# Opening an attention layer by scale alone: the norm's root and the shift moved behind the first six products

## The chip, the core and the metric

The kernel runs on one core of a Trainium2 chip. Its engines work side by side, each through its own list of instructions in order: TensorE (PE, matrix products into PSUM), VectorE (DVE), ScalarE (ACT), GpSimd (POOL), and SyncE (SP), which issues the DMAs of this kernel. The metric is the device time of one execution in microseconds (us); lower is better. The profile of one execution names every instruction by engine, line of the kernel, operation and tile.

## The reference

The model has two layers over 512 latent tokens and 256 context tokens of width 1024: grouped-query attention (16 query heads, 4 key heads, head dimension 64), then a gated feed-forward with a convolution, then a Mamba-2 style mixer, then another feed-forward. The change lies in the first few per cent of the time, at the start of the attention layer, where this is computed (cut to what matters):

```python
def rms_norm(x, g):                       # root over the 1024 features of a token
    return x * lax.rsqrt(jnp.mean(x * x, axis=-1, keepdims=True) + EPS) * g
def modulate(x, shift, scale):
    return x * (1 + scale) + shift
# shift, scale, gate: SiLU(cond) through a linear map of the layer (adaLN);
# latents use c, context tokens use c_ctx
h_lat = modulate(rms_norm(x,   g), shift_c,    scale_c)
h_ctx = modulate(rms_norm(ctx, g), shift_cctx, scale_cctx)
q_l, k_l, v_l = split(h_lat @ w_qkv)      # queries and keys are then normed per head (q_norm, k_norm)
q_c, k_c, v_c = split(h_ctx @ w_qkv)      # and the latents' rotated by position
```

All of it is in float32. For one token, with root r, gain a = g (1 + scale) and shift b, both vectors over the features: h = r (a x) + b, and so h W = r ((a x) W) + b W. The first form is what the kernel before computes; the second is what the changed kernel computes for the first six tiles of keys and queries.

## The kernel before

**Layout.** Features lie on the 128 partitions, tokens along the free axis. X holds the stream as eight feature tiles of 128 x 768 (512 latents, then 256 context tokens). A float32 product is made as three fp32r products (`mm3`, lines 104, 105 and 107): high part of the weight by high part of the activation, high weight by low activation, low weight by high activation. So every operand is first split: the high part is a copy rounded to fp32r, the low part is the difference. For weights `split` does it (L85 on ACT, L87 on DVE or POOL), for activations `modulated` does (L321 on DVE: x times gain times root into `ht`; L330 on ACT: plus shift, rounded, the high part; L331 on DVE: the low part). With `pool=True` it is L326 and L327 on ACT and L328 on POOL instead of the last two.

**The opening** is in `attention()`. There a block under `manual_schedule` (L523 to L639) keeps PE, ACT and DVE in the order in which the code is written. First X is loaded (L1570), the squares are summed (L574 on ACT, L576 on DVE), and `rstd_rows` makes the root of each token and spreads it over the partitions (from L274 on). Only then come eight steps, one per feature tile m. Step m needs

- the shift and the gain of tile m: `ada` multiplies 1 MB of adaLN weights (DMA `wada`, products `ps_ada` L128), copies them (`ada_sb`, L130), turns them (`ps_adt`, L134), and `modulation` makes `mod` (L145, shift and scale) and `moda` (L148, gain times one plus scale);
- a slab of weights, 128 x 768 (DMA into `wst`, then `wsh` on ACT L85 and `wsl` on POOL L87, the last on DVE);
- the two halves `hha`, `hla` of the modulated latents of tile m.

Then 18 products of 512 columns add tile m to six PSUM tiles `ps_l`: two tiles of keys and the first four of queries. From m = 4 on, two tiles of the context are modulated behind each step's latents (`pool=True`), with a root made at m = 3 and 4 from `sqc`.

**Behind the opening** the order is set by the priorities of the program rather than by hand. The six `ps_l` are copied to `raw` (L646, ACT). Six context products `ps_c` of 24 instructions each follow with the same slabs, each copied behind the latents' columns of `raw` (L863). A finished `raw` tile goes through the head norm and the rotation: squares `qsq` (L671, ACT), norm weight (L672, ACT), four small DMAs `qsw` that swap pairs (L675), sums `ssq` (L680, PE), cosine and sine (L682 to L684, DVE), root (L689 to L691, ACT), L693 to L695 (DVE). Then keys and queries are split, the values `ps_v` (L660) and the first score maxima `ps_m` (L764) are computed, and the heads follow one after the other for the rest of the layer. The values and the later queries read the same modulated latents `hha`, `hla`.

Of the kernel before, what the change touches and what calls it, by code (L numbers as in the profile page):

```python
# [7 lines left out]
P = 128  # L8
# [7 lines left out]
D = 1024  # L16
# [36 lines left out]
_col("cc", 2 * KT)  # L53
_col("qn", 1)
_col("kn", 1)
# [240 lines left out]

def parts(x, a=0, b=1 << 30):
# [217 lines left out]
def attention(g, adas, project, X):  # L515
# [6 lines left out]
    g.h = [[htiles(g, n, f"a{i}_{m}") for m in range(KT)] for i, n in enumerate((L, C))]  # L522
    hl, hc = g.h  # L523
# [32 lines left out]
    nc.sync.dma_start(g.cst, I["cst"][:, :CST_COS])  # L556
    for m in range(1, 5):
        next(mods[m])
        next(loads[m])
        if m == 2:  # L560
            for a in range(0, KT, 4):
                nc.sync.dma_start(X[:, a : a + 4, L:], I["ctxT"][a * P : (a + 4) * P].rearrange("(k p) t -> p k t", p=P))
# [7 lines left out]
    busy(38)  # L570
    acc = t3(g, "acc", n=L)
    for m in range(KT):
        sq = t2("sql") if m else acc
        nc.scalar.activation(sq, xs[0][m], AF.Square)  # L574
# [14 lines left out]
    next(norm)  # L589
    next(mods[0])  # L590
    busy(8)
    rsl, _, _ = next(norm)
    next(mods[0])
    next(loads[0], None)
    busy(3)
    modulated(g, hl[0], xs[0], rsl, 0, L, 0, 1, 0, 0, 0)
    rs_ps, rsl = rsl, t3(g, "rsl", n=L)
    nc.scalar.copy(rsl, rs_ps)
# [7 lines left out]
    for m in range(KT):  # L606
# [3 lines left out]
        if m == 1:  # L610
            sqc = t3(g, "sqc", n=C)
# [1121 lines left out]
```

## Time and profile before

| what | us |
|---|---|
| median of 3 runs | 1885.04 |
| lowest and highest of them | 1882.46, 1888.78 |
| the profiled execution's own time | 1889.8 |
| its span from first to last instruction | 1888.0 |
| PE busy in the span | 1862.3 |

The granted clock of TensorE is 0.995 of full speed over that execution. The profiled execution lies 4.8 us above the median of the runs, so a length read in the trace is compared with the profiled execution's own time, and differences are carried over to the median. In the rows of a timeline the first number is the start in us from the start of the span, the second the length; then come engine, line, operation, output and inputs with their shapes and the count. In square brackets stands the time the engine idled just before, and what ended it.

The opening runs until about 65 us, the context products until about 89 us, and the first score maxima start at 96.31 us. All that follows, 95% of the time, is the same code in both kernels, but for two details: the context's tiles now hold both halves in one tile, and the second mixer loads its input into tiles of that size.

### The profile page before, as it was taken

Reading aid. Unit: us, or ns where it says so; the run is one execution under the profiler, and the core shown is the slowest. Engines: PE = TensorE matmul, PEld = TensorE weight load, DVE = VectorE, ACT = ScalarE, POOL = GpSimd, SP = SyncE. Lnnn points to the kernel's source line nnn. Section 1 sums busy time; section 2 is a strip of 40 time slices with the busy share of each in tenths; the row PEclk is TensorE's granted clock in tenths of the full one; section 3 lists DMA queues with packets and bytes.
Section 4 is the critical chain, followed back from the end, with each engine's and each line's share of the span. In section 5 each row is a group of like instructions: output and inputs, shape, how many; then the busy total and the mean of one; then the engine's idle time right before and its main releaser. Section 6 shows DMA issues by size and latency. Waiting matters only on the chain.

```text
span 1888.0 us, 27471 instructions
## 1 busy us (share of the span) xinstructions
PE 1862.3 (99%) x10794; PEld 1535.3 (81%) x10794; DVE 1346.3 (71%) x2013; ACT 832.8 (44%) x1422; POOL 251.8 (13%) x220
## 2 busy tenths in 40 slices
PE   9999999999999999999999999999999999999999
PEld 7865555689888888888898888888887888888887
DVE  5688899678777777444478977777888576565655
ACT  3655544354122222222256677766667352323331
POOL 2100000030000000000030435454434200000000
PEclk9999999989999999999999999999999999999999
DMA  9223241024443555222223344343344323323232
GB/s 342 68 83 114 89 145 62 2 78 145 156 124 121 171 188 167 68 68 67 80 77 106 91 123 133 104 133 123 108 129 136 97 74 105 101 83 107 90 101 90
DMA packets 73489, 210.02 MB, mean 111 GB/s; under 512 B 8976, under 2 KB 14480, under 8 KB 73232
## 3 DMA queue, kind: packets, MB, share of 16 engines
q1 hardware_dynamic: 73360, 208.26, 34.8%
q8 instruction: 85, 1.39, 0.3%
q14 instruction: 44, 0.36, 0.1%
HBM read 198.79 MB, written 6.82 MB: 109 GB/s over the span
## 4 chain that ended last, share of the span: by engine, by line
PE 84%; DVE 7%; DMA 3%; ACT 3%; issue 2%; SPq 1%; POOL 1%; DVEq 0%; POOLq 0%; ACTq 0%
PE ps_up L104 10%; PE ps_up L105 10%; PE ps_up L107 10%; PE ps_d L104 6%; PE ps_d L107 6%; PE ps_d L105 6%; PE ps_in L104 4%; PE ps_in L105 4%; PE ps_in L107 4%; PE ps_o L802 2%; PE ps_s L838 2%; PE ps_st L1348 1%; PE ps_wo L105 1%; PE ps_wo L107 1%; PE ps_wo L104 1%
## 5 line engine op out<-in xcount | busy, mean ns | idle before, releaser
L87 DVE TENSOR_TENSOR wl<-wst,wh 128x1024 fp32r<-128x1024 f32 x207 | 256.8, 1241 | 276.8 <-PE ps_up L105 114.2
L85 ACT CAST wh<-wst 128x1024 fp32r<-128x1024 f32 x207 | 216.9, 1048 | 440.6 <-DMA wst<-in_wup 319.5
L105 PE MATMUL ps_up<-hlf,wh 128*128 128x512 f32 x992 | 351.6, 354 | 0.0
L107 PE MATMUL ps_up<-hhf,wl 128*128 128x512 f32 x992 | 351.4, 354 | 0.0
L104 PE MATMUL ps_up<-hhf,wh 128*128 128x512 f32 x992 | 351.2, 355 | 0.0
L104 PEld LDWEIGHTS ps_up<-hhf,wh 128*128 128x128 f32 x992 | 187.5, 189 | 26.2
L105 PEld LDWEIGHTS ps_up<-hlf,wh 128*128 128x128 f32 x992 | 187.6, 189 | 26.1
L107 PEld LDWEIGHTS ps_up<-hhf,wl 128*128 128x128 f32 x992 | 187.4, 189 | 26.1
L104 PE MATMUL ps_in<-hhs,wh 128*128 128x512 f32 (+1 forms) x544 | 199.2, 366 | 0.5 <-ACT raw L1214 0.5
L107 PE MATMUL ps_in<-hhs,wl 128*128 128x512 f32 (+1 forms) x544 | 193.7, 356 | 0.0
L105 PE MATMUL ps_in<-hls,wh 128*128 128x512 f32 (+1 forms) x544 | 193.6, 356 | 0.0
L107 PE MATMUL ps_d<-hdh,wl 128*128 128x512 f32 (+1 forms) x496 | 173.4, 350 | 0.0
L104 PE MATMUL ps_d<-hdh,wh 128*128 128x512 f32 (+1 forms) x496 | 173.3, 350 | 0.1
L105 PE MATMUL ps_d<-hdl,wh 128*128 128x512 f32 (+1 forms) x496 | 172.9, 349 | 0.0
L1030 DVE SCALAR_TENSOR_TENSOR X<-ps_d,mod,X 128x256 f32<-128x256 f32 (+1 forms) x176 | 102.5, 612 | 27.1 <-PE ps_d L107 26.8
L104 PEld LDWEIGHTS ps_in<-hhs,wh 128*128 128x128 f32 x544 | 102.8, 189 | 15.3 <-issue 1.0
L107 PEld LDWEIGHTS ps_in<-hhs,wl 128*128 128x128 f32 x544 | 102.7, 189 | 14.8
L105 PEld LDWEIGHTS ps_in<-hls,wh 128*128 128x128 f32 x544 | 102.9, 189 | 13.0
L105 PEld LDWEIGHTS ps_d<-hdl,wh 128*128 128x128 f32 x496 | 93.2, 188 | 14.4 <-DVE hdl L87 0.2
L107 PEld LDWEIGHTS ps_d<-hdh,wl 128*128 128x128 f32 x496 | 93.2, 188 | 13.1
L104 PEld LDWEIGHTS ps_d<-hdh,wh 128*128 128x128 f32 x496 | 93.0, 188 | 12.9 <-ACT hdh L85 0.3
L167 DVE SCALAR_TENSOR_TENSOR junk<-wada,cb 128x1024 f32<-128x1024 f32 x80 | 97.2, 1215 | 1.0 <-ACT cb L158 0.8
(389 smaller groups left out, 3668.1 us busy)
## 6 DMA issues: line engine op xcount, KB each, us to landing
wst<-in_wup SPq DMA_DIRECT2D x88, 512.0 KB, 3.6
wada<-in_adaT SPq DMA_DIRECT2D x56, 512.0 KB, 3.6
wst<-in_win SPq DMA_DIRECT2D x48, 512.0 KB, 3.6
wst<-in_wdown SPq DMA_DIRECT2D x44, 512.0 KB, 3.7
E<-ad SPq DMA_DIRECT2D x64, 256.0 KB, 6.8
wada<-in_adaB SPq DMA_DIRECT2D x24, 512.0 KB, 4.6
ec<-ead SPq DMA_DIRECT2D x64, 128.0 KB, 4.3
wst<-in_wout SPq DMA_DIRECT2D x16, 512.0 KB, 3.6
```

What stands on the lines that cost most here:

```text
L85: keep(nc.scalar.copy(hi, src))
L87: keep(eng.tensor_tensor(lo, src, _r(hi), ALU.subtract))
L104: mm(out, wh, ah, start=first, stop=False)
L105: mm(out, wh, al, start=False, stop=False)
L107: i = mm(out, wl, ah, start=False, stop=last)
L167: g.tc.keep_in_program_order(nc.vector.scalar_tensor_tensor(junk, w, 1.0, cb[:, v * D : (v + 1) * D], ALU.mult, ALU.mult, accum_out=md[:, ...
L802: nc.tensor.matmul(po[S64[e], :n], v, pr[:, 512 * e + off : 512 * e + off + n], start=first, stop=last)
L838: nc.tensor.matmul(outs[e], a[S64[e], k], b[S64[e], q], start=i == 0, stop=False)
L1030: nc.vector.scalar_tensor_tensor(ap, o[:, c0:c1], gate[:, m, v : v + 1], ap, ALU.mult, ALU.add)
L1348: nc.tensor.matmul(ps[:, d * 256 : (d + 1) * 256], Bt[:, t * P : (t + 1) * P], xw[d][t], start=t == ts[0], stop=t == ts[-1])
```

## The change

The changed kernel puts the latents into the six `ps_l` tiles as high and low part of gain times x: `scaled(m)` on ACT (L625 of the changed kernel) and DVE (L626). Neither root nor shift is in them, so X is loaded tile by tile between the adaLN weights and the slabs, and `par` (small parameters) is loaded in two pieces. The squares are summed during the steps (latents at m = 1 and 2, context at m = 3 and 4); `rstd_wide` makes the roots with one product against a matrix of ones, over 128 partitions at once, at m = 3 (latents, used from m = 4) and m = 5 (context, used from m = 6). The root is multiplied in on the way out of PSUM (L699, DVE, in the place of the copy L646). The shift enters as two more columns in each context tile (`shifts`, L631 and L632): the context products are 258 instead of 256 columns wide (`WX`), and the 257th column of the result, copied to `wb` (L920), is added to `raw` (L921, DVE). The context is modulated at m = 6 and 7, four tiles each, the odd ones by `pool=True`.

The values and the later queries still need fully modulated latents. `latent(m)` makes them: tile 0 at m = 5, tile 1 at m = 7, the other six behind the opening, odd ones with ACT and POOL.

```diff
-    g.h = [[htiles(g, n, f"a{i}_{m}") for m in range(KT)] for i, n in enumerate((L, C))]
-    hl, hc = g.h
+    hr = [htiles(g, L, f"r{m}") for m in range(KT)]
+    hl, hc = [], [pair_tile(g, f"hhc{m}") for m in range(KT)]
+    hc = [(t[:, :WX], t[:, WX:]) for t in hc]
...
+    x_in = lambda a, b: nc.sync.dma_start(X[:, a:b, :L], I["xT"][a * P : b * P].rearrange("(k p) t -> p k t", p=P))
+    nc.sync.dma_start(g.par[:, :NFIRST], I["par"][:, :NFIRST])
     next(mods[0])
+    nc.sync.dma_start(g.cst, I["cst"][:, :CST_COS])
     next(loads[0])
...
+    x_in(0, 1)
+    next(mods[1])
...
-    busy(38)
-    acc = t3(g, "acc", n=L)
-    for m in range(KT):
-        sq = t2("sql") if m else acc
-        nc.scalar.activation(sq, xs[0][m], AF.Square)
-        if m:
-            nc.vector.tensor_tensor(acc, acc, sq, ALU.add)
-    norm = rstd_rows(g, acc, L, g.ones[:, :1], D, "a", Bk)
...
+    def scaled(m):
+        gain = g.moda[0][1][:, m, 0:1]
+        hi, lo = hr[m]
+        nc.scalar.activation(hi, xs[0][m], AF.Identity, scale=gain)
+        nc.vector.scalar_tensor_tensor(lo, xs[0][m], gain, _r(hi), ALU.mult, ALU.subtract)
+
+    def shifts(m):
+        b = g.mod[0][0][:, m, 0:1].broadcast_to([P, WX - C])
+        hi, lo = (t[:, C:] for t in hc[m])
+        nc.scalar.copy(hi, b)
+        nc.vector.tensor_tensor(lo, b, _r(hi), ALU.subtract)
...
+            k_step(m, j, pl[j], hr)
...
+                    scaled(m + 1)
+            if j == 2 and m in (3, 5):
+                norm = rstd_wide(g, acc if m == 3 else sqc, t2, Bk)
+            if j == 2 and m in (3, 4, 5, 6):
+                next(norm, None)
...
+            if j == 3 and m >= 6:
+                for a in range(4 * m - 24, 4 * m - 20):
+                    modulated(g, tuple(t[:, :C] for t in hc[a]), xs[1], sqc, 0, C, 0, 1, 0, 1, a, pool=a % 2)
+                    shifts(a)
+            if j == 4 and m in (5, 7):
+                latent(len(hl))
...
     for j in range(6):
-        nc.scalar.copy(raw[j][:, :L], pl[j])
+        nc.vector.tensor_tensor(raw[j][:, :L], pl[j], acc, ALU.mult)
+    for m in range(len(hl), KT):
+        latent(m, m % 2)
...
-            k_step(k, j, ps[:, :C], hc)
+            k_step(k, j, ps[:, :WX], hc)
         nc.scalar.copy(raw[j][:, L:], ps[:, :C])
+        b = g.p.tile([P, 2], F32, tag="rst", bufs=8, name="wb")
+        nc.scalar.copy(b, ps[:, C:WX])
+        nc.vector.tensor_scalar(raw[j][:, :L], raw[j][:, :L], b[:, 0:1], None, ALU.add)
```

New functions, as they stand in the changed kernel (`busy`, the products that fill the wait at the start, drops from 38, 8 and 3 to 14, 2 and 7):

```python
def rstd_wide(g, sq, tile, bank):
    nc = g.nc
    n = sq.shape[-1]
    ps = bank("ssa")[:, :n]
    nc.tensor.matmul(ps, g.ones, sq, start=True, stop=True)
    a, y, u = (tile(nm)[:, :n] for nm in ("rsa", "rsy", "rsu"))
    nc.vector.tensor_scalar(a, ps, 1.0 / D, EPS, ALU.mult, ALU.add)
    nc.scalar.activation(y, a, AF.Ln)
    nc.scalar.activation(y, y, AF.Exp, scale=-0.5)
    yield
    nc.vector.tensor_tensor(u, y, a, ALU.mult)
    nc.vector.scalar_tensor_tensor(u, y, -0.5, u, ALU.mult, ALU.mult)
    nc.vector.scalar_tensor_tensor(sq, u, 1.5, y, ALU.add, ALU.mult)
```

Three places show how the order of the instructions moves. The first is SP's list of loads at the very start, before and now.

```order
L1570 DMA X<-in_xT 128x2x512 x4
L1571 DMA par<-in_par 128x548
L122 DMA wada<-in_adaA 128x768 x2
L122 DMA wada<-in_adaA 128x512
L547 DMA wst<-in_wslab 128x768
L556 DMA cst<-in_cst 128x132
```

```order
L584 DMA par<-in_par 128x74
L126 DMA wada<-in_adaA 128x768 x2
L126 DMA wada<-in_adaA 128x512
L586 DMA cst<-in_cst 128x132
L576 DMA wst<-in_wslab 128x768
L583 DMA X<-in_xT 128x512
```

The 2 MB of X stood ahead of everything; now the adaLN weights of tile 0 do, and one tile of X stands behind the first slab.

The second place is DVE between the last low part of a latent tile (`hla_7`, now `hlr`) and the first instruction on the finished tile 0 of `raw` (`raw_738` before, `raw_696` now; L682 is the cosine).

```order
L321 SCALAR_TENSOR_TENSOR ht<-X,moda_98,rsl 128x512
L331 SCALAR_TENSOR_TENSOR hla_7_117<-ht,mod_86,hha_7_116 128x512
L321 SCALAR_TENSOR_TENSOR ht<-X,moda_98,rsc 128x256 x4
L87 TENSOR_TENSOR wl<-wst,wh 128x1024
L682 TENSOR_TENSOR raw_738<-raw_738,cs 128x512
```

```order
L626 SCALAR_TENSOR_TENSOR hlr_112<-X,moda_93,hhr_111 128x512
L313 TENSOR_TENSOR rsu<-rsy,rsa 128x256
L314 SCALAR_TENSOR_TENSOR rsu<-rsy,rsu 128x256
L315 SCALAR_TENSOR_TENSOR sqc<-rsu,rsy 128x256
L349 SCALAR_TENSOR_TENSOR ht<-X,moda_93,sqc 128x256
L359 SCALAR_TENSOR_TENSOR hhc_113<-ht,mod_81,hhc_113 128x256
L632 TENSOR_TENSOR hhc_113<-mod_81,hhc_113 128x2
L349 SCALAR_TENSOR_TENSOR ht<-X,moda_93,sqc 128x256
L632 TENSOR_TENSOR hhc_114<-mod_81,hhc_114 128x2
```

The last five of these rows, for one even and one odd context tile, come four times, for `hhc_113` to `hhc_120` (L349 is the former L321, L359 the former L331). Behind them, still ahead of the cosine of `raw_696`, DVE has these:

```order
L632 TENSOR_TENSOR hhc_120<-mod_81,hhc_120 128x2
L349 SCALAR_TENSOR_TENSOR ht<-X,moda_93,acc 128x512
L699 TENSOR_TENSOR raw_696<-ps_l,acc 128x512
L699 TENSOR_TENSOR raw_697<-ps_l,acc 128x512
L359 SCALAR_TENSOR_TENSOR hla_686<-ht,mod_81,hha_685 128x512
L699 TENSOR_TENSOR raw_698<-ps_l,acc 128x512
L699 TENSOR_TENSOR raw_699<-ps_l,acc 128x512
L699 TENSOR_TENSOR raw_700<-ps_l,acc 128x512
L699 TENSOR_TENSOR raw_701<-ps_l,acc 128x512
L349 SCALAR_TENSOR_TENSOR ht<-X,moda_93,acc 128x512 x3
L359 SCALAR_TENSOR_TENSOR hla_709<-ht,mod_81,hha_708 128x512
L921 TENSOR_SCALAR raw_696<-raw_696,wb 128x512
```

So the modulation of the context, the way out of PSUM and the modulated latents 1 to 4 now stand on DVE between the last `hlr` and the addition that completes `raw_696`. Three more rows L349, two L359, one L921 and the low part of a weight follow before the cosine.

The third place is ACT around the squares of the first finished tile (`qsq`, L671 before, L726 now), which the first head norm waits for.

```order
L646 COPY raw_742<-ps_l 128x512
L646 COPY raw_743<-ps_l 128x512
L863 COPY raw_738<-ps_c 128x256
L671 ACTIVATE qsq<-raw_738 128x768
L672 ACTIVATE raw_738<-raw_738,kn 128x768
```

```order
L920 COPY wb<-ps_c 128x2
L89 CAST wh<-wst 128x1024
L358 ACTIVATE hha_708<-ht,mod_81 128x512
L354 ACTIVATE ht<-ht,mod_81 128x512
L355 CAST hha_714<-ht 128x512
L358 ACTIVATE hha_721<-ht,mod_81 128x512
L354 ACTIVATE ht<-ht,mod_81 128x512
L355 CAST hha_727<-ht 128x512
L358 ACTIVATE hha_734<-ht,mod_81 128x512
L726 ACTIVATE qsq<-raw_696 128x768
L354 ACTIVATE ht<-ht,mod_81 128x512
L727 ACTIVATE raw_696<-raw_696,kn 128x768
```

The squares were the next instruction behind the copies; now the high parts of latents 2 to 6 stand ahead of them. PE's list behind the opening keeps its order: two context products of 24 instructions each (now interleaved with each other, before the first of them partly with the last step), the sums `ssq` of the first `raw` tile, the third context product, the sums of the second tile, the other three, the values, the first maxima.

More of the change, by code (lines that the diff above doesn't have):

```diff
@@ L52 @@
 _col("dtb", 1)
-_col("cc", 2 * KT)
-_col("qn", 1)
-_col("kn", 1)
 NPAR = _n
@@ L553, in attention @@
     xs = [[X[:, m, c0:c1] for m in range(KT)] for c0, c1 in ((0, L), (L, T))]
+    x_in = lambda a, b: nc.sync.dma_start(X[:, a:b, :L], I["xT"][a * P : b * P].rearrange("(k p) t -> p k t", p=P))
+    nc.sync.dma_start(g.par[:, :NFIRST], I["par"][:, :NFIRST])
     next(mods[0])
+    nc.sync.dma_start(g.cst, I["cst"][:, :CST_COS])
     next(loads[0])
[L556 to L562, printed above, removed]
+    x_in(0, 1)
+    next(mods[1])
+    x_in(1, 2)
+    next(loads[1])
+    next(mods[2])
+    x_in(2, 4)
+    next(loads[2])
+    x_in(4, 6)
+    next(mods[3])
+    next(loads[3])
+    x_in(6, 8)
+    nc.sync.dma_start(g.par[:, NFIRST:], I["par"][:, NFIRST:])
+    next(mods[4])
+    next(loads[4])
+    for a in range(0, KT, 4):
+        nc.sync.dma_start(X[:, a : a + 4, L:], I["ctxT"][a * P : (a + 4) * P].rearrange("(k p) t -> p k t", p=P))
     warm = Bk("warm")
@@ L588, in attention, with squared, latent @@
                             e.rearrange("p (k v) -> p k v", v=2), ALU.mult)
-    next(norm)
+    g.qn8 = g.const.tile([P, 1], F32, name="qn8")
+    nc.vector.tensor_scalar(g.qn8, g.par[:, PC["qn"] : PC["qn"] + 1], -0.5 / HD * HD ** -0.5, None, ALU.mult)
+    kn = g.const.tile([P, 1], F32, name="kn")
+    nc.vector.tensor_scalar(kn, g.par[:, PC["kn"] : PC["kn"] + 1], -0.5 / HD, None, ALU.mult)
+    def scaled(m):
[8 more added lines that the diff above has]
+        nc.vector.tensor_tensor(lo, b, _r(hi), ALU.subtract)
+    def squared(acc, x, first):
+        sq = t2("sq")[:, : x.shape[-1]] if first else acc
+        nc.scalar.activation(sq, x, AF.Square)
+        if first:
+            nc.vector.tensor_tensor(acc, acc, sq, ALU.add)
+    def latent(m, pool=False):
+        hl.append(htiles(g, L, f"a{m}"))
+        modulated(g, hl[m], xs[0], acc, 0, L, 0, 1, 0, 0, m, pool=pool)
+    busy(14)
     next(mods[0])
-    busy(8)
-    rsl, _, _ = next(norm)
+    busy(2)
+    next(loads[0], None)
     next(mods[0])
[L594 to L598, printed above, removed]
+    scaled(0)
+    busy(7)
     pl = [Sb("ps_l") for _ in range(2)]
@@ L1456, in ssd @@
         prev = cur
-    xn = [[g.p.tile([P, C], F32, tag="h256", bufs=16, name=f"x{m}{i}") for i in range(2)] for m in range(KT)]
+    xn = [[t[:, :C], t[:, C : 2 * C]] for t in (g.p.tile([P, 2 * WX], F32, tag=f"h{C}", bufs=8, name=f"x{m}") for m in range(KT))]
     for m in range(KT):
@@ L1568, in body @@
     g.par = g.const.tile([P, NPAR], F32, name="par")
-    for m in range(0, KT, 2):
-        nc.sync.dma_start(X[:, m : m + 2, :L], I["xT"][m * P : (m + 2) * P].rearrange("(k p) t -> p k t", p=P))
-    nc.sync.dma_start(g.par, I["par"])
     g.ident, g.blk, g.sel = (cst[:, a:b] for a, b in
```

62 lines of the change are left out of this document (32 added, 30 removed).

## The prediction

> **What bounds the kernel now.** I read the page first (busy time of each engine, the chain of waits by engine), then the chain in the first 100 us, then the timeline from the first product to the first score maxima, then busy time by stretch.
>
> ```profile
> PE 1862.3 (99%) x10794; PEld 1535.3 (81%) x10794; DVE 1346.3 (71%) x2013; ACT 832.8 (44%) x1422; POOL 251.8 (13%) x220
> PE 84%; DVE 7%; DMA 3%; ACT 3%; issue 2%; SPq 1%; POOL 1%; DVEq 0%; POOLq 0%; ACTq 0%
> ```
>
> TensorE is busy 99% of the span and 84% of the chain. So what happens in the opening shifts everything behind it by the same time: I only have to find when the first score maxima start. In the chain, the opening begins with three loads (start, length):
>
> ```profile
> 1.73 5.85 DMA X<-in_xT
> 7.60 7.10 DMA wada<-in_adaA
> 14.71 9.15 DMA X<-in_ctxT
> ```
>
> ```profile
> 18.26 0.50 PE L104 MATMUL ps_l<-hha,wsh 128*128 128x512 f32 x1 [0.28 <-ACT hha L330]
> 64.41 0.75 DVE L331 SCALAR_TENSOR_TENSOR hla<-ht,mod,hha 128x512 fp32r<-128x512 f32 x1 [0.79 <-ACT hha L330]
> 72.04 0.85 ACT L671 ACTIVATE qsq<-raw 128x768 f32<-128x768 f32 x1
> 80.74 0.39 PE L104 MATMUL ps_c<-hha,wsh 128*128 128x256 f32 x1 [0.56 <-DVE qsq L693]
> 96.31 0.50 PE L764 MATMUL ps_m<-kh,qh 64*128 64x256 f32 x4
> ```
>
> These five rows are my marks: first product, last low part of the latents, squares of the first finished `raw` tile, first product of the fourth context tile (it waits for the head norm), first maxima. Between them, by stretch (us, then busy time and count of PE, PEld, DVE, ACT, POOL; then granted clock, DMA share, GB/s):
>
> ```profile
> 32.00:34.00 2.00, 0.69 (x3) 0.20 (x2) 1.95 (x2) 0.00 (x0) 1.33 (x1) 1.00 1.04 405
> 36.00:38.00 2.00, 2.00 (x6) 1.60 (x5) 0.75 (x1) 0.61 (x1) 0.00 (x0) 0.50 1.02 395
> 52.00:66.00 14.00, 13.60 (x83) 10.23 (x76) 8.50 (x18) 6.46 (x13) 4.82 (x5) 1.00 0.00 0
> 66.00:74.00 8.00, 7.66 (x52) 6.81 (x50) 0.74 (x2) 7.70 (x17) 2.98 (x4) 1.00 0.01 3
> ```
>
> From 52 to 74 us PE idles 0.7 us of 22: it is the bound there, and the context's modulation is hidden under it. DVE has room in the last row (0.74 of 8), ACT has none (7.70).
>
> **Part 1: the first product comes earlier.**
>
> ```profile
> 4.64 0.63 ACT L574 ACTIVATE acc<-X 128x512 f32<-128x512 f32 x1 [2.32 <-DMA X<-in_xT]
> 23.95 1.34 ACT L615 ACTIVATE sqc<-X 128x256 f32<-128x256 f32 x4 [0.92 <-DMA X<-in_ctxT]
> 12.38 1.07 PE L128 MATMUL ps_ada<-wada,sc 128*32 128x256 f32 x16
> 14.16 0.41 DVE L130 COPY ada_sb<-ps_ada 128x256 f32<-128x256 f32 x1
> 15.71 0.51 PE L134 MATMUL ps_adt<-cst,ada_sb 128*128 128x2 f32 x4
> 17.49 0.72 ACT L330 ACTIVATE hha<-ht,mod 128x512 fp32r<-128x512 f32 x1 [3.11 <-DVE ht L321]
> 13.55 0.83 ACT L85 CAST wsh<-wst 128x768 fp32r<-128x768 f32 x1 [0.42 <-DMA wst<-in_wslab]
> 16.51 0.16 DVE L148 SCALAR_TENSOR_TENSOR moda<-mod,par 128x2 f32<-128x2 f32 x1
> 54.28 1.86 POOL L87 TENSOR_TENSOR wsl<-wst,wsh 128x768 fp32r<-128x768 f32 x1
> 54.53 1.63 DVE L148 SCALAR_TENSOR_TENSOR moda<-mod,par 128x2 f32<-128x2 f32 x1
> ```
>
> By the issue order 0.52 MB had landed at 4.64 us and 7.82 MB at 23.95 us: 7.30 MB in 19.3 us, 0.38 MB/us. In the new order `par`'s first part and the adaLN weights of tile 0 make 1.09 MB: landed at 4.64 + 0.56/0.38 = 6.1 us, the first slab (1.55 MB) at 7.4. Then 1.07 for `ps_ada`, 0.41 for its copy, 0.51 for the turn: 8.15 us. ACT splits the slab from 7.4 to 8.2; POOL makes its low part until 10.05. The last two rows show what that does to DVE: `moda`, a 128x2 operation of 0.16 us the row before, took 1.63 us there and ended at 56.16, when POOL's 1.86 us that began before it ended, at 56.14. I read it as DVE held up by POOL whenever both read two SBUF tensors. So `moda` of tile 0 ends at 10.2, the high part 0.72 later: first product at 11.0 (9.4 without the hold-up), **7.3 us earlier**. The 15 MB of the opening need 15/0.38 = 40 us as before; step 7's weights land at about 43 and are needed after 50, so the loads stay covered.
>
> [...]
>
> **Part 2: the steps.**
>
> ```profile
> 46.38 0.50 PE L104 MATMUL ps_l<-hha,wsh 128*128 128x512 f32 x1
> 52.22 0.50 PE L104 MATMUL ps_l<-hha,wsh 128*128 128x512 f32 x1
> L693 DVE SCALAR_TENSOR_TENSOR qsq<-ssq,qsq 128x512 f32<-128x512 f32 x10 | 6.9, 689 | 3.5 <-ACT qsq L691 2.6 <-issue 0.8
> L680 PE MATMUL ssq<-qsq,ones 64*64 64x512 f32 x12 | 3.2, 614 | 0.0
> ```
>
> A step is 5.84 us (52.22 − 46.38); eight, without the 1.07 of a ninth tile's adaLN, are 45.6. The `scaled` pair costs ACT and DVE no more than the old pair, and the old first operation `ht` falls away. Two wide root products are added; the trace has none of 128 rows: 0.61 us (last row, half the rows) to twice that for the latents, half of it for the context, 0.9 to 1.8 together; I take 1.3. The squares need 12 x 0.69 us on DVE or less, spread over steps 1 to 4 under 5.84 us each: hidden. In step 5 DVE has the root's three operations (3 x 0.69) and the context's sums ahead of `ada_sb`, which the next step waits for: 2.5 us, from 0 if it hides. So the last `ps_l` product ends at 11.0 + 45.6 + 1.3 + 2.5 = 60.4. The last low part is made during the step before: step 6 starts at 60.4 − 4.2 (18 products) − 5.84 = 50.4, and its adaLN, turn, POOL-free slab split and `scaled` pair put `hlr` at 55.4, against 65.16 before. **The lead is then 9.8 us.**
>
> **Part 3: the context on DVE's list.**
>
> ```profile
> 51.10 0.87 DVE L321 SCALAR_TENSOR_TENSOR ht<-X,moda,rsc 128x256 f32<-128x256 f32 x2
> 51.67 0.51 ACT L326 ACTIVATE ht<-ht,mod 128x256 f32<-128x256 f32 x1 [1.27 <-DVE ht L321]
> 52.22 0.41 ACT L327 CAST hha<-ht 128x256 fp32r<-128x256 f32 x1
> 52.70 1.60 POOL L328 TENSOR_TENSOR hla<-ht,hha 128x256 fp32r<-128x256 f32 x2 [4.19 <-ACT hha L327]
> L330 ACT ACTIVATE hhf<-ht,mod 128x256 fp32r<-128x256 f32 x36 | 17.1, 504 | 11.7 <-DVE ht L321 11.6
> L331 DVE SCALAR_TENSOR_TENSOR hlf<-ht,mod,hhf 128x256 fp32r<-128x256 f32 x36 | 16.5, 477 | 0.2 <-ACT hhf L330 0.2
> ```
>
> Here the order decides. Before, DVE ran ahead: two `ht` back to back (0.87), the rest on ACT and POOL. Now each even tile's low part stands on DVE *ahead of the next tile's* `ht`, and the two-column operation of an odd tile behind ACT's two passes. DVE waits for ACT in every tile: even 0.44 + 0.50 + 0.48 + 0.1 = 1.5 us; odd 0.44 + 0.51 + 0.41, then the two-column operation, held up until POOL's 0.80 is through: 2.3 to 2.4. (An operation of two columns I count 0.1 to 0.2, by the 0.16 of `moda`; POOL's 0.80 is half of the fourth row.) Four pairs make 15.8 us, 12.6 without POOL's hold. With the root's three operations (3 x 0.43 = 1.3) the last tile is complete at 55.4 + 1.3 + 15.8 = 72.5. PE is through with `ps_l` at 60.4 and then follows tile by tile: 24 products of two context tiles, 5.5 us of work in 12 us.
>
> **Part 4: the way out of PSUM and the latents.**
>
> ```profile
> L1172 DVE TENSOR_SCALAR dtu<-dte 128x384 f32<-128x384 f32 x1 | 0.4, 360 | 0.9 <-ACT dte L1170 0.9
> 77.93 0.69 DVE L682 TENSOR_TENSOR raw<-raw,cs 128x512 f32<-128x512 f32 x1 [1.04 <-DMA qsw<-raw]
> ```
>
> Before, six copies on ACT. Now DVE has six multiplications out of PSUM (no such row; nearest L693, 0.69 with one input in PSUM; bounds 0.41, the copy L130, and 0.75; taken 0.65), and mixed with them, by the order, five `ht` of 512 columns (0.75 each, as L331), two low parts, and the addition (0.36 x 512/384 = 0.48) before the first `raw` tile is whole: 6 x 0.65 + 5 x 0.75 + 2 x 0.75 + 0.48 = 9.6, less starts that overlap; then ACT's high part of latent 6, ahead of `qsq`, waits for two more `ht` and a low part on DVE, one of them held up by POOL's low parts. I take 11.1 us on DVE and 0.72 on ACT (bounds 7 if ACT reaches `qsq` early, 13 if POOL holds twice): `qsq` at 72.5 + 11.1 + 0.7 = 84.3, **12.3 us later** than 72.04.
>
> From there the rows run as before (swap by DMA, sums, root: 8.70 us from 72.04 to 80.74), with an addition and a low part between: + 0.6. The fourth context tile starts at 80.74 + 12.9 = 93.7 and, as 72 context and 60 value products follow as before (15.57 us to the maxima), the maxima at 109.2: **+12.9 us**. Two extra columns on 256 (under 1% of 17 us of products) I leave out; the loads of `adaA` no longer delay anything there, `cs` and `wv` land while DVE is busy. [...] Forecast **+11**: 1889.8 + 11 = 1900.8 for the profiled execution, and, this lying 4.8 above the median, 1885.04 + 11 = **1896**.
>
> **Rivals.** *No hold-up by POOL.* The same list, with odd tiles 1.5 instead of 2.4 us, and 1 to 2 us less in part 4: +3 to +7, about 1890.5. For it: POOL's 0.80 a tile is short, and a hold costs only where DVE stands ready in just that moment. Against: the 1.63 us of `moda`.
>
> ```profile
> 89.19 7.19 PE ps_v L660 x60
> 74.20 1.51 PE L680 MATMUL ssq<-qsq,ones 64*64 64x512 f32 x8
> ```
>
> *The lead survives.* If the context's last high part is ready before PE ends `ps_l` (60.4) and `qsq` runs before 67, PE never idles: 11.0 + 45.6 + 1.3 + 16.9 (six context tiles, three of which take 89.19 − 80.74 = 8.45) + 3.0 (two sums of 1.51) + 7.2 (values) = 85.0 instead of 96.31, −11; with up to half of it lost, −6 to −11, about 1876. For it: PE is 99% busy, so 7.3 us of it removed at the front should show; DVE is idle 7 of 8 us from 66 to 74. Against: 15.8 us of context on DVE and ACT begin at 56.7, behind the steps, where before they were spread over four steps.
>
> *The clock on top.* In the row at 32 us PE idled 1.3 of 2 us, and at 36 the granted clock was 0.50. After some 20 us with gaps the products from 84 on could run at half clock for some us: 1.5 to 5 more, +16 to +20, about 1903. [...]
>
> *It cancels, or does not do what it says:* the loads set the pace of the first steps (their margin is about 2 us in steps 1 to 4), or the lead and the tail come out alike: within 3 us, 1885.
>
> **How the numbers follow.** Forecast (+8 to +15) 0.58; no hold-up 0.17; lead survives 0.13; clock 0.07; cancels 0.05. A measurement of this kernel can tell about 0.3%, 5.7 us. Slower: 0.58 + 0.07 + half of 0.17 = 0.74; within: the other half and 0.05 = 0.13; faster 0.13. The forecast's own range is 1891 to 1901; the range for 8 in 10 reaches through the no-hold-up case to cancelling, 1884, and up to 1902.
>
> **What would show it.** First product near 11 us, last low part `hlr` near 55: parts 1 and 2. PE idle more than 10 us between 60 and 85, ended by DVE and ACT on `hhc` and `ssq`: part 3. Rows L632 of 0.8 us ending with POOL's: the hold-up. `qsq` (L726) at 84: part 4. If PE is busy through 60 to 85, or `qsq` stands before 72, I am wrong, and the kernel is faster.

## The result, and the profile after

The changed kernel takes 1908.33 us (median of 6 runs, 1906.15 to 1911.15) against 1886.09 us of the kernel before (6 runs, 1882.46 to 1888.78): a ratio of 1.0118, 95% interval 1.0103 to 1.0134, so 22 us slower (19 to 25). The forecast was slower by 11, range to 1902. The direction came out; the size is double, and the time lies outside the range.

The profiled execution took 1907.13 us with a span of 1905.3. Two lines of its page, busy time by engine and the chain of waits by engine:

```profile
PE 1859.7 (98%) x10728; PEld 1526.2 (80%) x10728; DVE 1363.7 (72%) x2042; ACT 838.4 (44%) x1435; POOL 259.7 (14%) x219
PE 78%; DVE 11%; issue 5%; DMA 2%; POOL 2%; ACT 1%; SPq 0%; DVEq 0%; POOLq 0%; ACTq 0%
```

TensorE has as much work as before (1862.3 us), but its part of the chain fell from 84 to 78%, and DVE's rose from 7 to 11%. The timeline of the same execution at the five marks of the prediction (start, length; lines are those of the changed kernel):

```profile
10.17 0.48 PE L108 MATMUL ps_l<-hhr,wsh 128*128 128x512 f32 x1
61.64 0.75 DVE L626 SCALAR_TENSOR_TENSOR hlr<-X,moda,hhr 128x512 fp32r<-128x512 f32 x1 [0.80 <-ACT hhr L625]
91.69 0.83 ACT L726 ACTIVATE qsq<-raw 128x768 f32<-128x768 f32 x1
101.20 0.40 PE L108 MATMUL ps_c<-hhc,wsh 128*128 128x258 f32 x1 [0.81 <-DVE qsq L748]
117.44 0.50 PE L819 MATMUL ps_m<-kh,qh 64*128 64x256 f32 x4
```

The first product stands 8.1 us earlier, the last low part only 2.8 us earlier (62.39 against 65.16), the squares 19.7 us later, the first maxima 21.1 us later. The loss is all there at the maxima: at the first `ps_up` product (442.85 before, 463.83 now) the two profiled executions still stand 21.0 us apart. At their ends it is 17.3, where the medians differ by 22. TensorE's wait in between, by stretch (us, then busy time and count of PE, PEld, DVE, ACT, POOL; granted clock, DMA share, GB/s):

```profile
78.00:82.00 4.00, 1.41 (x6) 0.94 (x6) 3.86 (x7) 2.44 (x8) 0.73 (x1) 0.67 0.00 0
82.00:86.00 4.00, 0.00 (x0) 0.00 (x0) 4.00 (x7) 1.51 (x3) 0.00 (x0) 0.50 0.00 0
86.00:90.00 4.00, 0.00 (x0) 0.00 (x0) 2.84 (x5) 2.46 (x4) 3.43 (x2) 0.50 0.00 0
90.00:94.00 4.00, 1.43 (x4) 0.52 (x6) 3.88 (x5) 2.94 (x5) 0.47 (x1) 0.50 0.00 0
```

TensorE does next to nothing for 13 us, while DVE works with one break of 1.2 us. What delayed DVE's list so far stands earlier, in the steps:

```profile
29.59 4.56 DVE L638 TENSOR_TENSOR acc<-acc,sq 128x512 f32<-128x512 f32 x4
31.77 1.83 POOL L91 TENSOR_TENSOR wsl<-wst,wsh 128x768 fp32r<-128x768 f32 x1 [3.66 <-ACT wsh L89]
34.53 0.63 PE L138 MATMUL ps_adt<-cst,ada_sb 128*128 128x2 f32 x4 [1.60 <-DVE ada_sb L134]
36.46 1.91 PE L307 MATMUL ssa<-acc,ones 128*128 128x512 f32 x2
47.76 1.88 POOL L91 TENSOR_TENSOR wsl<-wst,wsh 128x768 fp32r<-128x768 f32 x1 [3.42 <-ACT wsh L89]
47.88 3.63 DVE L638 TENSOR_TENSOR sqc<-sqc,sq 128x256 f32<-128x256 f32 x4
51.90 0.91 PE L138 MATMUL ps_adt<-cst,ada_sb 128*128 128x2 f32 x4 [2.78 <-DVE ada_sb L134]
```

Four additions of 512 columns took 4.56 us, with POOL's 1.83 us inside them; four of 256 took 3.63 with POOL's 1.88 beside them, from 0.1 us before. In each block one addition alone waited: 2.17 us instead of 0.69, and 2.04 instead of 0.43. Behind them in DVE's list stands the copy `ada_sb`, and TensorE waited 1.6 and 2.8 us for it. Each of these two waits is followed by a stretch at half clock; a third wait for `ada_sb`, 0.9 us at 26.82, is not:

```profile
36.00:38.00 2.00, 2.00 (x5) 1.00 (x3) 0.75 (x1) 0.39 (x1) 0.00 (x0) 0.50 1.03 393
52.00:54.00 2.00, 2.00 (x7) 1.81 (x8) 0.39 (x3) 0.69 (x1) 0.00 (x0) 0.51 0.00 0
```

### The profile page after: what moved, and what is told of

It is laid out like the page before. It is cut to its first block, busy times and chain, and to the rows that moved or that the text cites. A ratio compares the mean times of both kernels' runs of the same rounds, so it can differ in the third digit from the quotient of the medians.

```text
span 1905.3 us, 27384 instructions
## 1 busy us (share of the span) xinstructions
PE 1859.7 (98%) x10728; PEld 1526.2 (80%) x10728; DVE 1363.7 (72%) x2042; ACT 838.4 (44%) x1435; POOL 259.7 (14%) x219
## 4 chain that ended last, share of the span: by engine, by line
PE 78%; DVE 11%; issue 5%; DMA 2%; POOL 2%; ACT 1%; SPq 0%; DVEq 0%; POOLq 0%; ACTq 0%
PE ps_up L111 10%; PE ps_up L108 10%; PE ps_up L109 10%; PE ps_d L108 6%; PE ps_d L111 5%; PE ps_d L109 5%; PE ps_in L108 3%; PE ps_in L111 3%; PE ps_in L109 3%; PE ps_o L857 2%; PE ps_s L893 2%; DVE xf L1278 2%; PE ps_wo L109 1%; PE ps_wo L111 1%; PE ps_wo L108 1%
## 5 line engine op out<-in xcount | busy, mean ns | idle before, releaser
L109 PE MATMUL ps_up<-hlf,wh 128*128 128x512 f32 x664 | 258.8, 390 | 0.0
L109 PEld LDWEIGHTS ps_up<-hlf,wh 128*128 128x128 f32 x664 | 124.6, 188 | 24.8
L109 PE MATMUL ps_in<-hls,wh 128*128 128x512 f32 x368 | 143.8, 391 | 0.0
L108 PEld LDWEIGHTS ps_d<-hdh,wh 128*128 128x128 f32 x496 | 92.9, 188 | 12.9 <-ACT hdh L89 0.3
L896 ACT ACTIVATE pr<-ps_s 128x1024 f32<-128x1024 f32 x56 | 57.1, 1020 | 87.1 <-PE ps_s L895 87.0
```

Of the source, the lines that this page charges most:

```text
L108: mm(out, wh, ah, start=first, stop=False)
L109: mm(out, wh, al, start=False, stop=False)
L896: nc.scalar.activation(pr, ps, AF.Exp)
```

## The experiments

**Theories.** The first is the prediction's, extended by the rows just shown: DVE works through its list in order, and the time is one chain of four terms on it. These are the steps up to the last `hlr`, the context's tiles, the way to the squares `qsq`, and the stretch from there to the first maxima. In the steps the sums of the squares stand ahead of the copy, and POOL's low parts hold DVE up. The rivals: the loads or TensorE's clock set the pace of the steps; the amount of work rather than its order makes the context slow; the latents cost the same wherever they stand; the low clock behind the waits costs the rest.

Each run below was timed in three rounds, that called lean with early latents in five, against the kernel before on the same chip. The table gives the time by its ratio to that kernel, and the four terms from each run's own trace: end of the last `hlr`; from there to the last two-column operation on `hhc`; from there to the start of `qsq`; from there to the first maxima. (In the plans the last rows of the context stand among other work.)

| kernel | ratio (95% interval) | last `hlr` | context | to `qsq` | to maxima | first maxima |
|---|---|---|---|---|---|---|
| changed | 1.0118 (1.0103 to 1.0134) | 62.39 | 16.45 | 12.85 | 25.75 | 117.44 |
| squares in gaps | 1.0102 (1.0085 to 1.0119) | **59.42** | 16.35 | 13.08 | 26.22 | 115.07 |
| slabs' low parts on DVE | 1.0081 (1.0064 to 1.0099) | **55.69** | 16.38 | 13.09 | 25.66 | 110.82 |
| context in phases | 1.0074 (1.0053 to 1.0094) | 60.41 | **9.60** | 12.87 | 25.75 | 108.63 |
| context without POOL | 1.0089 (1.0066 to 1.0113) | 62.97 | **13.62** | 12.87 | 26.18 | 115.64 |
| latents late | 1.0087 (1.0063 to 1.0111) | 60.87 | 16.45 | **5.61** | 28.34 | 111.27 |
| filler, 34 products | 1.0126 (1.0110 to 1.0141) | 61.96 | 16.43 | 14.74 | **24.70** | 117.83 |
| three orders together | 1.0054 (1.0033 to 1.0074) | 57.90 | 9.56 | 5.34 | 28.07 | 100.87 |
| plan | 1.0064 (1.0040 to 1.0088) | 59.44 | 8.81 | 3.46 | 27.56 | 99.27 |
| plan without POOL | 1.0047 (1.0033 to 1.0060) | 56.09 | 7.23 | 4.02 | 28.91 | 96.25 |
| lean plan, latents late | 1.0062 (1.0047 to 1.0078) | 55.74 | 7.23 | 4.58 | 27.96 | 95.51 |
| lean plan, latents early | 1.0050 (1.0037 to 1.0062) | 55.93 | 7.23 | 4.60 | 33.41 | 101.17 |
| plan, no second latents | 0.9989 (0.9976 to 1.0002) | 55.70 | 7.23 | 4.02 | 25.31 | 92.26 |

Where the steps are left as in the changed kernel, the last `hlr` ends between 60.4 and 63.0 us (61.7 in the mean of six); that is how far one trace of that term can be trusted. TensorE's clock goes with this spread. Over the window from 12 to 60 us the mean granted clock is 0.96 in the two traces that end at 60.4 and 60.9 (context in phases, latents late), and 0.93 in the four that end at 61.6 to 63.0. The other terms repeat to some tenths.

### Squares in the gaps

```diff
-            if j == 3 and m in (1, 2):
-                for a in range(4 * m - 4, 4 * m):
-                    squared(acc, xs[0][a], a)
-            if j == 3 and m in (3, 4): ... squared(sqc, xs[1][a], a)   # four of them
+            if j == 3 and m in (1, 2):
+                squared(acc, xs[0][3 * m - 1], 1)
...
                     next(loads[m + 1], None)
+                    if m in (1, 2, 3): squared(acc, xs[0][a], a)      # a = 3m - 3, 3m - 2
+                    if m in (4, 5): squared(sqc, xs[1][a], a)         # four of them
```

> The changed kernel with the sums of the squares moved to the gap on DVE behind each step's copy of the adaLN product (two latent tiles a step behind it and one at the old place, in steps 1 to 3; four context tiles behind it in steps 4 and 5), where they stood in blocks of three or four ahead of that copy. If the sums on DVE's list were what stretched the steps (PE waited 0.9 + 1.6 + 2.8 us for the copy), the last low part hlr moves from 62.4 to about 57.5 and the first maxima from 117.5 to about 113: 4 to 6 us less than the changed kernel. If the loads or TensorE's clock set the pace of the steps, less than 1 us.

The last `hlr` came at 59.42, 2.3 us below the mean of the unchanged steps, the maxima 2.4 us earlier; the ratio's interval overlaps that of the changed kernel. The clock over the steps was 0.96 here, and against the two traces of the unchanged steps with the same clock the last `hlr` gains only 1.2 us. The order of the sums is a part of the stretch at best, and at most half of what was expected. The timeline on DVE tells why:

```profile
31.74 2.69 DVE L638 TENSOR_TENSOR acc<-acc,sq 128x512 f32<-128x512 f32 x2 [0.16 <-ACT sq L636]
44.79 2.21 DVE L314 SCALAR_TENSOR_TENSOR rsu<-rsy,rsu 128x512 f32<-128x512 f32 x1
```

Two additions of 0.7 us took 2.69, and one operation of the root, 0.69 us in the changed kernel, took 2.21: outside the blocks too, DVE's operations on two SBUF tensors were held up. Without POOL in the steps they are not: two additions in the same gap take 1.48 us in the plan without POOL (at 32.38) against 2.71 in the plan with it (at 31.61), and the root's operation takes 0.69 in the run that follows (at 43.08).

### Slabs' low parts on DVE

```diff
-        split(g, st, hi, lo, lo_engine="pool" if k < 7 else "dve")
+        split(g, st, hi, lo, lo_engine="dve")
```

> The changed kernel with the low parts of all eight slabs on DVE (0.95 us each) instead of POOL (1.85) in the first seven; nothing else is moved. If POOL's operations held up DVE in the steps (moda 1.64, the sums 4.56 and 3.63 us with POOL's 1.83 inside them), the time from the second to the last high part hhr falls from 42 to 44 us to about 40, although DVE gets 6.7 us more to do, and the first maxima come 2 to 4 us earlier. If the holds are harmless, the steps get longer by what DVE has more, 1 to 4 us.

This is the largest single repair of the steps. From the second to the last high part `hhr` it took 37.0 us (17.15 to 54.18) instead of 44.4 (16.45 to 60.88) in the changed kernel, more than expected, although DVE got 6.7 us more to do. The maxima came 6.6 us earlier. The same blocks of sums, in the same place, on DVE's timeline of this run:

```profile
29.10 3.07 DVE L638 TENSOR_TENSOR acc<-acc,sq 128x512 f32<-128x512 f32 x4
44.41 2.01 DVE L638 TENSOR_TENSOR sqc<-sqc,sq 128x256 f32<-128x256 f32 x4
```

3.07 instead of 4.56, and 2.01 instead of 3.63. Without POOL the blocks of sums, in their old place, no longer stretch the steps much: a step of the kernel before is 5.84 us, six of them are 35.0, and the root's two products take 1.02 and 0.59 us on TensorE in this run's timeline (1.91 and 1.05 in the changed kernel's, at half the clock). So the hold-up by POOL, not the order of the sums, was the greater part of the miss. TensorE in the steps (columns as above), first in the changed kernel, then in this run:

```profile
12.00:60.00 48.00, 42.68 (x255) 28.86 (x254) 27.57 (x53) 19.09 (x34) 11.36 (x6) 0.93 0.74 278
12.00:60.00 48.00, 46.52 (x285) 32.45 (x286) 31.04 (x71) 21.48 (x40) 0.00 (x0) 1.00 0.74 280
```

TensorE's idle time fell from 5.3 to 1.5 us, and the clock rose from 0.93 to 1.00; 0.07 of 48 us are 3.4 us of full clock. The two together make 7.2 of the 7.4 us. That POOL's low part simply came too late for TensorE is ruled out by the changed kernel's trace: there no wait of TensorE in the steps was ended by `wsl`.

The loads, the first of the rivals, stand close behind. In the changed kernel's chain no load appears between the first product and the last `hlr`. In this run the chain runs back through loads until 37.0 us, with the squares in gaps until 37.8 us. So with the holds gone the first half of the steps goes at the pace of the loads.

### Context in phases, and context without POOL

```diff
-                for a in range(4 * m - 24, 4 * m - 20):
-                    modulated(...sqc..., a, pool=a % 2)
-                    shifts(a)
+                gens = [modulated_in_steps(...sqc..., a, pool=a % 2) for a in range(4 * m - 24, 4 * m - 20)]
+                # all four ht, then ACT's passes, then the low parts, then shifts of all four
```

> The changed kernel with the context's modulation issued in phases for four tiles at a time: four ht, then the high parts, then the low parts and the two-column operations; the same operations on the same engines. If DVE and ACT waiting for each other in every tile makes the 16.4 us from the last hlr to the last context tile, they shrink to about 8.5, and the first maxima come 7 to 8 us earlier. If the amount of work on ACT, DVE or POOL sets it, less than 2 us.

The context's term fell from 16.45 to 9.60 with the same operations on the same engines, and the maxima came 8.8 us earlier (two of these from the steps' spread, here with the clock at 0.96). DVE's timeline, first four tiles:

```profile
61.70 1.67 DVE L368 SCALAR_TENSOR_TENSOR ht<-X,moda,sqc 128x256 f32<-128x256 f32 x4
63.29 0.48 DVE L381 SCALAR_TENSOR_TENSOR hhc<-ht,mod,hhc 128x256 fp32r<-128x256 f32 x1
64.06 0.65 DVE L381 SCALAR_TENSOR_TENSOR hhc<-ht,mod,hhc 128x256 fp32r<-128x256 f32 x1 [0.29 <-ACT hhc L379]
64.99 0.91 DVE L653 TENSOR_TENSOR hhc<-mod,hhc 128x2 fp32r<-128x2 f32 x4 [0.28 <-ACT hhc L652]
```

The second kernel of this pair keeps the order and takes POOL out of the context (`pool=a % 2` becomes no argument, so all tiles go the even tiles' way).

> The changed kernel with all eight context tiles modulated by DVE and ACT, none by POOL; the order is left as it is. If POOL's low part holds up the two-column operation on DVE (0.70 us instead of 0.15 in the trace, behind ACT's two passes), an odd tile costs 1.55 us instead of 2.25 and the first maxima come about 3 us earlier, although DVE has more to do. If POOL only takes work off DVE, it is 0 to 2 us later.

The term fell by 2.83 us, to 13.62. An odd tile's end in the changed kernel:

```profile
66.81 0.73 POOL L356 TENSOR_TENSOR hhc<-ht,hhc 128x256 fp32r<-128x256 f32 x1 [17.17 <-ACT hhc L355]
66.86 0.70 DVE L632 TENSOR_TENSOR hhc<-mod,hhc 128x2 fp32r<-128x2 f32 x1 [1.16 <-ACT hhc L631]
```

and in this run:

```profile
66.86 0.49 DVE L359 SCALAR_TENSOR_TENSOR hhc<-ht,mod,hhc 128x256 fp32r<-128x256 f32 x1 [0.58 <-ACT hhc L358]
67.26 0.15 DVE L632 TENSOR_TENSOR hhc<-mod,hhc 128x2 fp32r<-128x2 f32 x1
```

An operation on two columns, 0.15 us by itself, took 0.70 beside POOL's low part of 0.73. The maxima came 1.8 us earlier in this trace, and the whole time can't tell: 1.0089 against 1.0118, intervals that overlap.

### Latents late

```diff
-    for m in range(len(hl), KT):
-        latent(m, m % 2)
...
-        for t in range(T // P):
+        for t in (4, 5, 0, 1, 2, 3):          # values of the context first
...
         for gen in early:
             next(gen, None)
+        for _ in range((0, 1, 1, 1, 1, 2)[n]):
+            latent(len(hl), len(hl) % 2)
```

> The changed kernel with the modulated latents 2 to 7 issued during the context products, behind the first head norm's squares, and the values of the context tokens computed ahead of those of the latents. If their place ahead of the squares makes the 12.9 us from the last context tile to qsq, these become about 5.5 and the first maxima come 5 to 7 us earlier. If they only come back as a wait ahead of the values or the maxima, or DVE is the bound there, 0 to 2 us.

The way to the squares fell from 12.85 to 5.61, as expected, and the maxima came 6.2 us earlier. ACT's and DVE's timeline now have the squares right behind the shift:

```profile
82.42 0.88 DVE L919 TENSOR_SCALAR raw<-raw,wb 128x512 f32<-128x512 f32 x2
82.93 0.84 ACT L724 ACTIVATE qsq<-raw 128x768 f32<-128x768 f32 x1 [2.28 <-DVE raw L919]
```

But 2.6 us of it came back between the squares and the maxima (28.34 instead of 25.75), and more behind them: the last value product started at 129.2 us, 4.0 us earlier than in the changed kernel (133.2), not 6.2; and 1.5 of these are the steps' spread (60.87 against 62.39). So both theories have a part: the place is worth 2.5 to 4 us, the rest returns as work.

### The three orders together

> The changed kernel with three edits of order together: squares in the gaps behind the copy, context in phases of four tiles, latents 2 to 7 behind the first squares. If the three are terms of one chain they add up: last hlr about 59.5, context 9.6 later, qsq 5.6 after that at about 75, first maxima at 101 to 103, the time 5 to 8 us above the kernel before and 14 to 17 below the changed kernel. If they hide one another, the gain over the best of them alone (context in phases, maxima at 108.6) is under 3 us.

The terms add up: 57.90, 9.56, 5.34, and the maxima at 100.87, just ahead of the expected 101 to 103, 16.6 us ahead of the changed kernel and 4.6 behind the kernel before. The clock helped: it was 1.00 over the steps, against 0.93 in the changed kernel. The time does not follow all the way: 10 us above the kernel before (ratio 1.0054) where 5 to 8 were expected. The last value product stood at 118.8, 6.7 us behind the kernel before (112.1).

### The filler products

```diff
         nc.vector.tensor_scalar(raw[j][:, :L], raw[j][:, :L], b[:, 0:1], None, ALU.add)
+        if n == 1:
+            for _ in range(34):               # 70 in the first of the two runs
+                nc.tensor.matmul(warm[:, :P], g.ones, raw[j][:, L : L + P], start=True, stop=True)
```

> The changed kernel with 70 products of 128 columns more on TensorE, on finished context columns, in the wait between the second context product and the sums of the squares (79 to 91.7 us); their results are not used. If the lower granted clock after that wait (0.50 until 94 us, 0.70 until 98) costs time, qsq stays at about 91.7 and the stretch from qsq to the first maxima, 25.8 us, becomes 24 or less: 1.5 to 3 us. If the clock costs nothing there, the stretch stays and the products only fill idle time.

The 70 products were too many: they took 15.9 us and held the sums `ssq` back until 101.14, 8.6 us behind the changed kernel, and the kernel was slower (ratio 1.0152, 1.0132 to 1.0173). Hence the second:

> As the run with 70 products more, which took some 19 us and held up the sums of the squares, but with 34, enough for the wait from 82 to 91.7 us. If the lower clock behind the wait costs time, the stretch from qsq to the first maxima shrinks from 25.8 to about 23.5 us and the kernel is 2 us faster than the changed kernel; if not, the stretch stays at 25.8.

The clock stayed up (1.00 from 86 to 102 us, where the changed kernel has 0.50 until 94 and 0.70 from 94 to 98), and the sums themselves were faster. First row: the changed kernel; second: this run.

```profile
92.57 2.82 PE L735 MATMUL ssq<-qsq,ones 64*64 64x512 f32 x8 [12.67 <-ACT qsq L726]
```

```profile
94.00 1.51 PE L735 MATMUL ssq<-qsq,ones 64*64 64x512 f32 x8 [0.50 <-ACT qsq L726]
```

The stretch from the squares to the maxima fell by 1.05 us, to 24.70, not by 2.3, and the time shows nothing (1.0126). The way to the squares was 1.9 us longer, because the filler moved more than the clock: the second context product ran behind the first instead of interleaved with it, so ACT's copy of it came at 85.22 instead of 80.49, and the latents' next high part, behind it in ACT's list, at 86.49 instead of 84.45. Halving the clock cost about 1 us between the squares and the maxima: the products behind `ssq` wait for the head norm on ACT and DVE anyway (0.81 us for `qsq` ahead of 101.20 in the changed kernel).

### The plans

The plan starts from phases and late latents and spreads the opening anew. The latents' squares lie in the gaps of steps 1 to 3, the context's in step 4; the context's root is in step 5, its tiles two, three and three in steps 5 to 7. The latents' root is in steps 6 and 7, and all eight modulated latents stand behind the first squares.

```diff
+            if j == 3 and m == 4: squared(sqc, xs[1][a], a)      # a = 4 to 7; 0 to 3 behind the copy
+            if j == 2 and m == 5: next(cnorm, None)
+            if j == 3 and m == 7: next(lnorm, None)
...
+            if j == 3 and m >= 5:
+                now = {5: (0, 1), 6: (2, 3, 4), 7: (5, 6, 7)}[m]  # in phases, then shifts
```

> The changed kernel planned anew: squares of the latents in the gaps of steps 1 to 3, of the context in step 4, the context's root in step 5, its tiles two, three and three in steps 5 to 7 in phases, the latents' root in steps 6 and 7, all eight modulated latents behind the first squares. If only the order on DVE kept the lead from the end, PE waits little between 60 and 70 us, qsq stands at about 68 and the first maxima at 93 to 97: at the kernel before or 1 to 4 us under it. If the work itself, moved from ACT to DVE, is too much for the opening, the maxima stay above 100.

> The same plan with no work for POOL in the opening: the low parts of all slabs (0.95 us instead of 1.85) and of the context on DVE. If POOL's operations hold up DVE for more than DVE itself needs for them, the steps get shorter and the maxima come 1 to 4 us ahead of the plan with POOL. If DVE is full in the steps, 1 to 4 us behind.

With POOL the maxima came at 99.27, between the two cases expected; without it at 96.25, level with the kernel before (96.31). Again POOL's absence is worth 3 us, here on the marks; the two ratios (1.0064, 1.0047) overlap. The squares stand at 67.34, 4.7 us *ahead* of the kernel before, and the time is still 9 us above it. So the opening is repaired, and something behind takes it away.

```diff
-        nc.vector.tensor_scalar(raw[j][:, :L], raw[j][:, :L], b[:, 0:1], None, ALU.add)
+        nc.scalar.activation(raw[j][:, :L], raw[j][:, :L], AF.Identity, bias=b[:, 0:1])
...
-            latent(len(hl), len(hl) % 2)
+            latent(len(hl))
```

> The plan without POOL in the opening, and with less work for DVE behind it: the shift is added on ACT (an activation with bias instead of DVE's 0.48 us, six times), the modulated latents without POOL, three of them issued with the first head norm, two with the next. If DVE's amount of work is what now keeps TensorE waiting (DVE busy 4.0 of 4 us from 90 to 102 in the plan without POOL, TensorE 2 of 4), the stretch with PE waits behind the values of the context shrinks by 5 to 9 us and the time comes within 3 us of the kernel before or below it. If the order alone, or the head norm's chain, keeps TensorE waiting, the gain over the plan without POOL is under 2 us.

> The same less work for DVE with the latents issued as late as in the plan without POOL (none, one, one, two, two, two per context product). If the amount of work on DVE sets the end, this gives 3 to 5 us over that plan and the earlier latents the rest; if the place of the latents does it, less than 2 us.

In both runs the first case of the expectation failed: less work for DVE gave nothing (1.0062 and 1.0050 against 1.0047). With early latents the maxima even moved back to 101.17. Their high parts now stand in ACT's list among the passes of the queries' root (one at 96.17, between two of them); that this is why is read from the list and not tested. What was left was the second modulation itself, its place and all its work together:

```diff
-            latent(len(hl), len(hl) % 2)
+    # hl[m] = hr[m]: values and later queries read the scaled parts
```

> The plan without POOL in the opening, with the modulated latents left out: values and later queries read the scaled high and low parts instead, so they lack root and shift. If making the latents a second time is what takes the lead away again behind the first head norm, the first maxima come at 88 to 92 us and the time is 2 to 6 us below the kernel before. If the head norm's own chain on ACT and DVE sets the end, the maxima stay at 95 or later and the time at or above the kernel before.

Without the second latents the maxima stand at 92.26, the last value product at 107.4, 4.7 us ahead of the kernel before, and the time is the same as the kernel before or a little under it (0.9989, 0.9976 to 1.0002). Against the plan it is based on that is 11 us, and the same end of the values: 118.9 there, 107.4 here. TensorE in the stretch to the maxima and in that of the values behind them (columns as above), first in the plan without POOL:

```profile
84.00:97.00 13.00, 9.32 (x70) 8.25 (x68) 12.93 (x16) 8.82 (x17) 3.69 (x2) 0.97 0.21 69
97.00:119.00 22.00, 18.62 (x110) 13.68 (x108) 17.00 (x22) 9.17 (x15) 2.93 (x2) 0.79 0.15 40
```

then in the run without the second latents:

```profile
84.00:93.00 9.00, 9.00 (x76) 8.61 (x74) 7.96 (x12) 6.60 (x12) 0.00 (x0) 1.00 0.29 102
93.00:108.00 15.00, 15.00 (x104) 11.68 (x105) 13.22 (x20) 4.45 (x10) 0.00 (x0) 1.00 0.13 31
```

DVE is full in the first row (12.93 of 13) and TensorE is idle 3.7 us of it; then 3.4 us more, at a clock of 0.79. The waits of both rows were ended by the second latents' halves `hha` and `hla` (3.7 us) and by ACT's `v` and `qh` (3.3 us). Without the latents TensorE is busy throughout at full clock.

The lead at the values does not last in this trace, which is that of the slowest of the run's ten executions. TensorE waits 2.0 us for the next head norm's squares (111.55) and 1.8 us for DVE (163.50), and the first product `ps_d` comes at 268.88, 3.4 us behind the kernel before (265.50). This run leaves work out that the result needs. So as an estimate, an order of these parts that keeps the second latents reaches at best what this run does, about the kernel before or up to 4.5 us under it; that no other order does better is not shown.

No version with the whole computation beat the kernel before.

## Where the prediction held and where it failed

**Part 1 (first product 7.3 us earlier, at 11.0):** right, at 10.17. The detail was not: `moda` of tile 0 came just ahead of POOL (9.05 against 9.17), and the low part behind it was the one held up, 1.53 us instead of 0.75. Which of the two comes first was luck. In four traces with this order of loads `moda` did, and the first product stood at 10.2 to 10.3. In five others POOL did, as the prediction assumed: `moda` took 1.24 to 1.78 us, and the first product stood at 11.6 to 12.0.

**Part 2 (the last low part at 55.4):** this step failed. It is the term of the steps, put at 45.6 + 1.3 + 2.5 with "hidden" for the squares; the last `hlr` came at 62.39, 7.0 us later, most of the 8.2 by which the first maxima missed the forecast of 109.2. The prediction had measured the hold-up by POOL, and used it for `moda` and for the context's odd tiles, but costed the sums of the squares at their bare 0.69 us. Yet these are operations on two SBUF tensors, at the time when POOL makes the slabs' low parts. The run with the slabs on DVE shows it: 37.0 us for six steps instead of 44.4 in the changed kernel, and the last `hlr` at 55.69, 0.3 us from where the prediction had put it. In the changed kernel TensorE waited 5.3 us for `ada_sb`, where the prediction had the 2.5 of step 5 alone, and lost 3.4 us to the clock, for which it had no term in the steps, although its own row at 36 us shows a clock of 0.50 there. The root's two products cost 2.56 us on the chain instead of 1.3 only because both fell into the half clock: in the run with the slabs on DVE, at full clock, their rows are 1.02 and 0.59 us long instead of 1.91 and 1.05.

**Part 3 (17.1 us from the last `hlr` to the last context tile):** right, 16.45. The sum had a few tenths too much: 1.5 and 2.3 to 2.4 us a pair make 15.2 to 15.6 for four, not 15.8. Both causes were named and both are shown: waiting tile by tile (9.60 in phases), and POOL's hold (13.62 without it). Its premise, that TensorE would wait for it, held too, 7 us later than forecast: TensorE idled 8.7 us between 60 and 85 us, and 16.3 until the sums at 92.57.

**Part 4 (11.8 us to the squares):** 12.85, right in kind. What was added for POOL is there in the timelines of DVE, ACT and POOL:

```profile
89.29 2.40 DVE L349 SCALAR_TENSOR_TENSOR ht<-X,moda,acc 128x512 f32<-128x512 f32 x2 [1.16 <-POOL hla L356]
91.06 0.72 ACT L358 ACTIVATE hha<-ht,mod 128x512 fp32r<-128x512 f32 x1 [2.18 <-DVE ht L349]
```

```profile
86.57 2.69 POOL L356 TENSOR_TENSOR hla<-ht,hha 128x512 fp32r<-128x512 f32 x1 [7.74 <-ACT hha L355]
```

**From the squares to the maxima (8.70 + 0.6 + 15.57 = 24.9):** 25.75, of which the filler run gives about 1 us to the clock.

**The forecast of +11** lies 2 us under the +12.9 that its parts add up to. No run shows these 2 us; where DVE came ahead of POOL, at `moda` of tile 0, its next operation was held (1.53 us instead of 0.75).

**The rivals.** That the lead survives fell with the squares at 91.69. The clock was counted only for the products behind the wait, where it costs about 1 us; it fell in the steps as well, where it cost 3.4. The case without POOL's hold-up is the opposite of what happened. The range ended at 1902 because the 7 us of Part 2 were in no case: "from 0 if it hides" was the only bound the sums had, and the upper one, each sum held by a POOL operation, was missing.

**What stays open.** The run with the slabs on DVE removes the hold-up and the half clock behind it together. Its trace puts 3.8 us on TensorE's waits and 3.4 on the clock, but no run changed the one without the other. Nor was a version tried in which values and later queries take root and shift on their way out as the first six tiles do, which is what the last run points to.

## What to carry to other kernels

A factor taken out of an operand and applied to the result frees the start only where the operand is used once: here the same tokens had to be modulated in full for other uses, and this second time cost about 11 us, more than the 8 us gained at the first product. When work is moved to a different place in an engine's list, cost each instruction with what runs beside it there, and carry a hold-up found in one row to every instruction of that kind, not only to the ones under discussion. The waits of an in-order engine for another, tile by tile, are removed by issuing the same work in phases over several tiles (16.45 to 9.60 us here). And before two traces are compared, their granted clocks over the stretch are: here one stretch of half clock more, 1.7 us, separates traces of the same steps.

## What the runs showed of the hardware

GpSimd was held up as well. Its low part of a 128x512 latent took 1.27 us where DVE was idle and 2.69 us at 86.57, while DVE went through an addition and two operations on two SBUF tensors one behind the other until 88.1; it ended 1.1 us after that. No row of the prediction shows this direction. On DVE the held operations ended with POOL's or just behind it: one of two columns ended at 67.56, POOL's at 67.54; one of 512 columns, begun at 31.97, ended at 34.15, 0.55 us behind POOL's 33.60. Operations with an input in PSUM were not held: inside POOL's 1.83 us from 42.51 the copy `ada_sb` took 0.42 us and the two operations `mod` 0.23 together; `moda` behind them, on two SBUF tensors, took 0.45 instead of 0.16 and ended at 44.36, POOL's at 44.35.

TensorE's granted clock fell to 0.50 behind waits of 1.6 and 2.8 us, each time for about 3.4 us, worked out from windows of 2 us (0.75, 0.50 and 0.90 from 34 us, 0.51 and 0.63 from 52). The length of the wait alone does not decide: in the run without POOL in the context the same wait of 1.60 us (before 35.07) left the clock at 1.00 (mean from 10 to 50 us).
